# Queries, keys and values of all heads in a first stage, kept in DRAM, instead of a projection inside every head's tiles

## The chip, the cores and the metric

The kernel runs on one core of one Trainium2 chip. The metric is device time in microseconds of one execution, the median of several runs. The trace is of one profiled execution of the kernel before. The granted TensorE clock in it is 1.000 over the whole span.

## The reference

One layer of an encoder over 1024 tokens of width 1024, all in float32. What matters here is branch B, a differential attention of 8 heads, each with two softmax maps of 64 channels and values of 128 channels:

```python
h = rmsnorm(x, g_mix[l])
z = h @ w_in[l]                      # 512 pooling columns | 1024 q | 1024 k | 1024 v
...
qn = head_rmsnorm(q, g_q) * (HEAD_DIM ** -0.5)
kn = head_rmsnorm(k, g_k)
...
    s = jnp.einsum('bqhid,bkhid->bihqk', qblk, kn)
    ...
    s = jnp.where(allowed, s + bias, neg)      # penalty by distance, block-causal mask
    p = jax.nn.softmax(s, axis=-1)
    a = p[:, 0] - lam * p[:, 1]
    return jnp.einsum('bhqk,bkhe->bqhe', a, vf)
...
o = head_rmsnorm(o, g_sub) * (1.0 - lambda_init)
...
gates = jax.nn.sigmoid(h @ w_gate[l] + b_gate[l])
merged = (gates[..., :D_MODEL] * (y_pool @ w_branch_pool[l])
          + gates[..., D_MODEL:] * (y_attn @ w_branch_attn[l]))
x = x + merged @ w_out[l]
```

Branch A is a pooling mixer over the first 512 columns of z. An MLP of width 4096 with a squared ReLU ends the layer.

## The kernel before

Every product of matrices is made of float32r operands that were split in a high and a low part (`split`), and takes three matmuls (`mm3`: hi·hi, hi·lo, lo·hi, lines 123 to 125). Below, z, sc, ta, tk, po, g and u are the names of PSUM tiles, that is, of what a matmul is for.

The tokens are in 8 tiles of 128. x is normalised and transposed to hT (split, kept in SBUF for the whole first part). Then a loop over all 64 pairs of head and tile, numbered g, runs a software pipeline. The string `O = "B1 C2 H6 D3 R7 E4 F5 W-2 A0"` names its stages and how many steps each lags:

- A, `stage_qkv`: the projection z of one tile for one head, 128 tokens by 384 columns (q, k, v of the head): 8 × 3 matmuls of 384 columns.
- B, `stage_prep`: squares and norms of q and k (ACT, DVE, POOL), and V split.
- C, `stage_qkT`: two transposes (tk, line 459) and the splits of K and Q in pieces of 64 partitions.
- D, `stage_scores`: scores sc (lines 499 and 500) in pieces of up to 512 keys. DVE evacuates each piece with the distance penalty and a running minimum (line 502), ACT takes the exponential with its sum (line 510), and DVE forms the coefficient (517, 518) and the difference of the two maps (519).
- E, `stage_aT`: transposes of the weights (ta, line 555), evacuated in halves hi and lo by ACT and DVE (lines 117, 118).
- F, `stage_pv`: the product with V for a pair of tiles (po).
- H, `stage_ssq`: the sum of squares of the outputs, with a 128 × 128 matrix of ones as the moving operand's partner (lines 590, 591) and a DVE pass (593).
- R, `stage_norm`: the factors of one head's outputs, to DRAM.
- W: the loads and splits of the next head's weights, `wqkv`.

A scheduler orders the instructions of each engine from this program. Gate columns (g, 16 units of two halves) and pooling groups (u, yp) are fillers: products without a deadline that are written behind the heads and are moved in where PE would have room. Their results go to DRAM (`g_dram`, `p_dram`). After the heads come the branch projections (bp, ba), w_out (op) and the MLP, itself by a Strassen scheme of seven products, which all stay as they are but for the rooms of some tiles.

## Time and profile before

| | us |
|---|---|
| median of 3 runs | 1554.02 (1553.6 to 1554.59) |
| the profiled execution | 1553.41 |
| its span | 1551.6 |
| PE busy in the span | 1533.6 (99%), 7649 matmuls |
| PEld (weight loads) | 1320.8 (85%) |
| DVE | 1011.3 (65%) |
| ACT | 816.7 (53%) |
| POOL | 354.8 (23%) |

The span goes from the first to the last instruction of the profiled execution; the time has 1.8 us around it. PE is TensorE's multiplies, PEld its weight loads, DVE the VectorE, ACT the ScalarE, POOL GpSimd, SP the engine that issues most of the DMAs. Busy times of matmuls overlap, so the busy time of a group on PE is more than what it takes of the span. In the groups, "out<-in" names the tiles, then come partitions × elements, the count, the busy time and the mean in ns of one, and the idle time ahead with what ended it.

### The profile page before, as it was taken

To read this page: it belongs to the slowest core of one execution; us is meant where nothing else is said; L and a number is where in the kernel's file an instruction comes from. 1 tells how busy PE (TensorE), PEld (TensorE's weight loads), DVE (VectorE), ACT (ScalarE), POOL (GpSimd) and SP (SyncE) were. 2 spreads that over 40 slices of the span, in tenths; PEclk is the share of its full clock that TensorE was granted. 3 is DMA by queue.
4 is the path that set the end of the run, shared out by engine and by line. 5 is a ranking of instruction groups with operands and counts; after the bars stand their busy time and mean duration, and the time that the engine had idled before them with its cause. 6 is when DMAs were issued, how large, how long until landed. Compare 5 with 4: busy or idle time off the path is not lost.

```text
span 1551.6 us, 22088 instructions
## 1 busy us (share of the span) xinstructions
PE 1533.6 (99%) x7649; PEld 1320.8 (85%) x7649; DVE 1011.3 (65%) x2277; ACT 816.7 (53%) x1810; POOL 354.8 (23%) x449
## 2 busy tenths in 40 slices
PE   7999999999999999999999999999999999999999
PEld 6999999999998989888888887888888788888887
DVE  7777677777878787746422458866665667556662
ACT  6656556656566555645532547565555633333331
POOL 5433334243525262324363400000000000000000
PEclk9999999999999999999999999999999999999999
DMA  7111212021202031248536534554343799437650
GB/s 229 51 53 48 66 41 68 24 75 37 75 28 83 28 96 42 69 147 284 179 122 210 168 112 124 182 185 155 129 142 109 278 334 370 170 122 257 224 190 27
DMA packets 168009, 206.94 MB, mean 133 GB/s; under 512 B 10117, under 2 KB 104026, under 8 KB 167898
## 3 DMA queue, kind: packets, MB, share of 16 engines
q1 hardware_dynamic: 150490, 178.23, 35.0%
q10 hardware_dynamic: 17408, 27.30, 4.7%
q8 instruction: 60, 0.98, 0.3%
q14 instruction: 51, 0.42, 0.1%
HBM read 150.94 MB, written 54.56 MB: 132 GB/s over the span
## 4 chain that ended last, share of the span: by engine, by line
PE 89%; DVE 4%; DMA 3%; ACT 1%; issue 1%; POOL 1%; SPq 0%; ACTq 0%; POOLq 0%; DVEq 0%
PE z L125 5%; PE z L123 5%; PE z L124 5%; PE Da L124 4%; PE Da L123 4%; PE Da L125 4%; PE g L123 3%; PE g L124 3%; PE g L125 3%; PE Db L124 3%; PE Db L123 3%; PE Db L125 3%; PE X L125 2%; PE X L123 2%; PE X L124 2%; PE sc L499 2%
## 5 line engine op out<-in xcount | busy, mean ns | idle before, releaser
L123 PE MATMUL z<-wqkv,hT 128*128 128x384 f32 x512 | 174.7, 342 | 0.4 <-DVE qn L441 0.3
L125 PE MATMUL z<-wqkv,hT 128*128 128x384 f32 x512 | 174.3, 341 | 0.5 <-DVE hT L118 0.5
L124 PE MATMUL z<-wqkv,hT 128*128 128x384 f32 x512 | 173.8, 339 | 0.0
L510 ACT ACTIVATE s<-s,nm 128x256 f32<-128x256 f32 (+7 forms) x128 | 99.6, 778 | 49.2 <-DVE nm L502 44.1
L249 POOL TENSOR_TENSOR ms<-ms,mhalf 128x4 f32<-128x4 f32 x64 | 66.6, 1040 | 157.7 <-DVE ms L248 139.1
L125 PE MATMUL g<-hT,fwgate 128*128 128x512 f32 x256 | 101.0, 394 | 0.0
L124 PE MATMUL g<-hT,fwgate 128*128 128x512 f32 x256 | 100.9, 394 | 0.0
L123 PE MATMUL g<-hT,fwgate 128*128 128x512 f32 x256 | 100.9, 395 | 0.0
L123 PEld LDWEIGHTS z<-wqkv,hT 128*128 128x128 f32 x512 | 96.9, 189 | 4.2 <-DVE qn L441 1.0
L125 PEld LDWEIGHTS z<-wqkv,hT 128*128 128x128 f32 x512 | 96.7, 189 | 3.3 <-DVE hT L118 1.3
L124 PEld LDWEIGHTS z<-wqkv,hT 128*128 128x128 f32 x512 | 96.8, 189 | 2.9
L502 DVE CUSTOM_DVE_ANT_0 s<-sc,dist 128x512 f32<-128x512 f32 (+3 forms) x128 | 74.7, 586 | 22.1 <-PE sc L500 20.7
L118 POOL TENSOR_TENSOR wqkv<-rqkv,wqkv 128x384 fp32r<-128x384 f32 x60 | 63.3, 1072 | 17.7 <-ACT wqkv L117 15.3
L499 PE MATMUL sc<-K,Q 128*128 128x512 f32 (+2 forms) x192 | 67.2, 355 | 0.1
L118 DVE TENSOR_TENSOR AS<-s,AS 128x512 fp32r<-128x512 f32 x64 | 43.8, 687 | 35.8 <-ACT AS L117 35.6
L500 PE MATMUL sc<-K,Q 128*128 128x512 f32 (+2 forms) x192 | 66.6, 354 | 0.0
L473 ACT CAST Q<-tk 64x128 fp32r<-64x128 f32 x128 | 33.2, 260 | 58.6 <-DVE Q L472 56.8
L447 POOL TENSOR_TENSOR qn<-qn,ggh 128x128 f32<-128x128 f32 x64 | 32.6, 510 | 137.5 <-DVE qn L441 124.2
L470 ACT CAST Q<-tk 64x128 fp32r<-64x128 f32 x128 | 33.1, 259 | 50.5 <-DVE K L469 49.1
L118 POOL TENSOR_TENSOR fwgate<-frgate,fwgate 128x512 fp32r<-128x512 f32 x32 | 45.2, 1416 | 52.2 <-ACT fwgate L117 52.0
L125 PEld LDWEIGHTS g<-hT,fwgate 128*128 128x128 f32 x256 | 48.1, 188 | 8.6
L123 PEld LDWEIGHTS g<-hT,fwgate 128*128 128x128 f32 x256 | 48.2, 188 | 7.1
(429 smaller groups left out, 4649.6 us busy)
## 6 DMA issues: line engine op xcount, KB each, us to landing
wd<-in_w_down_dram SPq DMA_DIRECT2D x56, 512.0 KB, 5.5
wu<-in_w_up_dram SPq DMA_DIRECT2D x32, 512.0 KB, 5.3
udS<-us SPq DMA_DIRECT2D x64, 256.0 KB, 2.5
ur<-udS SPq DMA_DIRECT2D x32, 512.0 KB, 3.2
rqkv<-in_w_in_dram SPq DMA_DIRECT2D x64, 192.0 KB, 2.8
ud<-u ACTq DMA_DIRECT2D x48, 256.0 KB, 2.2
ur<-ud SPq DMA_DIRECT2D x24, 512.0 KB, 5.5
frgate<-in_w_gate_dram SPq DMA_DIRECT2D x32, 256.0 KB, 2.6
```

What stands on the lines that cost most here:

```text
L118: return (lo_eng or nc.vector).tensor_tensor(lo, src, f(hi), op=ALU.subtract)
L123: nc.tensor.matmul(ps, lhs_hi, rhs_hi, start=first, stop=False, **kw)
L124: nc.tensor.matmul(ps, lhs_hi, rhs_lo, start=False, stop=False, **kw)
L125: nc.tensor.matmul(ps, lhs_lo, rhs_hi, start=False, stop=last, **kw)
L249: nc.gpsimd.tensor_tensor(dst, dst, mhalf[:, :n], op=ALU.pow)
L447: nc.gpsimd.tensor_tensor(qn[:, 2:4, :], qn[:, 2:4, :], ggh.unsqueeze(1).broadcast_to([P, 2, HD]), op=ALU.mult)
L470: nc.scalar.copy(q_hi, q)
L473: nc.scalar.copy(Q[other, m, 1, :], q)
L499: nc.tensor.matmul(dst, Q[:, i, 0, :], rhs, start=True, stop=False)
L500: nc.tensor.matmul(dst, Q[:, i, 1, :], rhs, start=False, stop=True)
L502: nc.vector.tensor_tensor_reduce(out=s[i][:, c : c + w], in0=sc[:, 0:w], in1=dist[:, o0 + c : o0 + c + w], scale=2.0 ** -(h + 1), scalar=B ...
L510: nc.scalar.activation(s[i][:, 0:n], s[i][:, 0:n], AF.Exp, bias=last, scale=-1.0, accum_out=Z[:, i, t : t + 1])
```

## The change

The loop over heads keeps scores, transposes, values' product and norms. What went before them (stages A, B, C, W) becomes a stage of its own, ahead of the heads and for all of them, through DRAM.

- **Values.** For two groups of four heads, each of the 8 tiles takes 24 matmuls of 512 columns. The result is split and stored in `v_dram`.
- **Queries and keys.** q and k of one head are two halves of an output of 256 rows by 1024 tokens; they are computed transposed (channels on partitions) with a scheme of seven products in place of eight. `comb` forms the sums T1 to T4 of quarters of hT once, on DVE, and `qk_pair` forms the sums S1 to S4 of the weights for each head. A product has 4 × 3 matmuls of 512 columns. They are kept in program order on PE (`pin`), two heads interleaved by the string `0111010010011`.
- **Norms.** The squares of a head's q and k are summed over channels with 16 matmuls of plain float32 (not float32r) and 2 columns against `bones`; the factors are transposed, go to DRAM (`rs_dram`) and come back broadcast (`rb`), are multiplied in, and K and Q are split and stored (`k_dram`, `q_dram`). The weights of a head from the fourth on are loaded only after the factors of the head three before it have been loaded.
- **Heads.** `O = "H3 D0 R4 E1 F2 Q-3 W-6"`: K and V come from DRAM six steps ahead (`head_start`), Q for a pair of tiles three steps ahead (`load_q`). The sums of squares of the outputs are two matmuls of plain float32 and 1 column for each pair of tiles. There are three score banks where there were two.
- **Fillers.** A unit u's weights are loaded after the Q load number `FILL(u)`, which spreads the 18 units over the heads' 32 pairs of tiles. They have two banks of their own, where before they had one and, for the last columns, z's. The gate's bias moves from the evacuation into the sigmoid.

The core of the diff:

```diff
-N_Z, N_S, N_T, N_F = 2, 2, 2, 1
+N_S, N_T, N_F = 3, 2, 2
...
+FILL = lambda u: min(max(u - 1, 0) * 4 * H // 18, 4 * H - 1)
...
-O = "B1 C2 H6 D3 R7 E4 F5 W-2 A0"
+O = "H3 D0 R4 E1 F2 Q-3 W-6"
...
+        def values(g, t):
+            th, c0 = t // 4, (t % 4) * P
+            ps = bankA("A", f"v{g}_{t}")
+            for k in range(NK):
+                mm3(
+                    ps, hT[k // 2, th, 0][:, k % 2, c0 : c0 + P], hT[k // 2, th, 1][:, k % 2, c0 : c0 + P],
+                    Wv[g, k][:, 0, :], Wv[g, k][:, 1, :], k == 0, k == NK - 1,
+                )
+            v = t4k(pv, "pb", [P, H // 2, 2, P], F32R, f"V{g}_{t}")
+            src = ps.rearrange("p (a b) -> p a b", a=H // 2)
+            split(v[:, :, 0, :], v[:, :, 1, :], src)
+            nc.scalar.dma_start(v_dram[g][:, :, t], f(v))
...
+                a, b, c = (temp(n) for n in "abc")
+                add(dve, a, f(B12[0]), f(B12[1]))
+                add(dve, b, f(B22[0]), f(B22[1]))
+                sub(dve, c, b, a)
+                keep_T(3, c)
...
+            def product(ps, a, b, more=False):
+                for k in range(4):
+                    mm3(ps, a[:, 0, k, :], a[:, 1, k, :], *operand(b, k), not more and k == 0, k == 3, more, pin)
+
+            with ExitStack() as order:
+                if h > 2:
+                    order.enter_context(tc.issue_after(rb_last[h - 3].ins))
+                (r11, r12), (r21, r22) = load(0), load(1)
...
+                sq = t4k(psq, "sq", [P, 512], F32, f"sq{h}_{th}{c is c2}")
+                nc.scalar.activation(sq, c[:, th, :], AF.Square)
+                o = 16 * (c is c2) + 4 * th
+                for j in range(4):
+                    pin(nc.tensor.matmul(
+                        ps[:, o + j : o + j + 9 : 8], sq[:, j * P : (j + 1) * P], bones, start=True, stop=True
+                    ))
...
+            for s, c in ((1, c2), (0, c1)):
+                rb = t4k(prb, "rb", [P, S], F32, f"rb{h}_{s}")
...
+                nc.sync.dma_start(f(K[i][0:HD]), d[0:4:3].rearrange("m p c -> p m c"))
...
+                nc.sync.dma_start(f(V[i]), v_dram[h // 4][:, h % 4, 4 * i : 4 * i + 4])
...
         def stage_ssq(h, p):
 
-            po, oq, oqs = st.pop((h, p, "o"))
-            nc.tensor.matmul(po[:, 256:512], ones, oqs[:, 0, :], start=True, stop=False)
-            nc.tensor.matmul(po[:, 256:512], ones, oqs[:, 1, :], start=False, stop=True)
...
+            po, oq = st.pop((h, p, "o"))
             for i in range(2):
...
+                nc.tensor.matmul(
+                    po[:, 256 + i : 257 + i], oq[:, i * P : (i + 1) * P], ones, start=True, stop=True
+                )
+            nc.scalar.copy(SS[h][:, 2 * p : 2 * p + 2], po[:, 256:258])
...
+        with ExitStack() as order:
+            if u > 1:
+                order.enter_context(tc.issue_after(q_loads[FILL(u)].ins))
+                order.enter_context(tc.issue_after(dist_set.ins))
+            return fill_cols(src, c0, name)
```

How the order of instructions moves, at three places. First TensorE among the first scores of head 2, in the kernel before (sc2_2_1_0 is head 2, tile 2, map 1, keys from 0; z2_6 is the projection of head 2, tile 6):

```order
L459 MATMUL tk2_3_2381<-identf_90,qn2_3_2270 128x128 x2
L555 MATMUL ta2_1_0_2408<-identf_90,s2_1_2289 128x128 x2
L500 MATMUL sc2_2_1_0_2417<-K2_0_1893,Q2_2_2276 128x384
L125 MATMUL z2_6_2555<-wqkv2_4_1701,hT2_1_1_326 128x384
L123 MATMUL z2_6_2555<-wqkv2_5_1704,hT2_1_0_325 128x384
L124 MATMUL z2_6_2555<-wqkv2_5_1704,hT2_1_0_325 128x384
L125 MATMUL z2_6_2555<-wqkv2_5_1704,hT2_1_1_326 128x384
L590 MATMUL po1_3_2303<-oqs1_3_2346,ones_97 128x256
L123 MATMUL z2_6_2555<-wqkv2_6_1710,hT3_1_0_327 128x384
L124 MATMUL z2_6_2555<-wqkv2_6_1710,hT3_1_0_327 128x384
L125 MATMUL z2_6_2555<-wqkv2_6_1710,hT3_1_1_328 128x384
L591 MATMUL po1_3_2303<-oqs1_3_2346,ones_97 128x256
```

The same place in the changed kernel, the head's tiles 1 to 3:

```order
L704 MATMUL sc2_1_0_0_3475<-Kb2_0_3146,Qb2_0_3287 128x256
L792 MATMUL po1_2_3386<-ones_76,oS1_2_3436 128x1 x2
L703 MATMUL sc2_1_1_0_3501<-Kb2_0_3146,Qb2_0_3287 128x256
L704 MATMUL sc2_1_1_0_3501<-Kb2_0_3146,Qb2_0_3287 128x256
L703 MATMUL sc2_2_0_0_3537<-Kb2_0_3146,Qb2_1_3393 128x384
L704 MATMUL sc2_2_0_0_3537<-Kb2_0_3146,Qb2_1_3393 128x384
L703 MATMUL sc2_2_1_0_3561<-Kb2_0_3146,Qb2_1_3393 128x384
L704 MATMUL sc2_2_1_0_3561<-Kb2_0_3146,Qb2_1_3393 128x384
L703 MATMUL sc2_3_0_0_3572<-Kb2_0_3146,Qb2_1_3393 128x512
L704 MATMUL sc2_3_0_0_3572<-Kb2_0_3146,Qb2_1_3393 128x512
```

The scores of several tiles now follow each other without a projection or a filler between them, and the sum of squares (line 792) is two products of one column. From the first score of head 2 to those of its tile 4 there were 213 rows of TensorE before, and there are 52 now: 24 scores' matmuls, 24 with values of head 1, four rows of transposes and one pair of squares' sums between them.

Second, VectorE in the new stage at the change from the first group of values to the second (comb and T are the sums of hT, wv1_4 is the lower half of the second group's weights for inner block 4, V0_7 that of the last tile's values):

```order
L116 TENSOR_TENSOR T3_01_781<-combc0_776,T3_00_780 128x1024
L116 TENSOR_TENSOR wv1_0_830<-rv1_0_739,wv1_0_830 128x512
L116 TENSOR_TENSOR wv1_1_833<-rv1_0_739,wv1_1_833 128x512
L232 TENSOR_TENSOR combb0_775<-combb0_775,comba0_774 128x1024
L116 TENSOR_TENSOR wv1_2_836<-rv1_1_742,wv1_2_836 128x512
L116 TENSOR_TENSOR wv1_3_839<-rv1_1_742,wv1_3_839 128x512
L229 TENSOR_TENSOR combe0_795<-hT2_0_0_236,hT2_0_1_237 128x1024
L116 TENSOR_TENSOR T1_01_787<-comba0_774,T1_00_786 128x1024
L116 TENSOR_TENSOR wv1_4_845<-rv1_2_842,wv1_4_845 128x512
L116 TENSOR_TENSOR wv1_5_848<-rv1_2_842,wv1_5_848 128x512
L116 TENSOR_TENSOR wv1_6_854<-rv1_3_851,wv1_6_854 128x512
```

The splits of the second group's weights stand among the sums of `comb`; none of this was there before.

Third, SP's queue at the end of the new stage, where the heads' first loads (Qb0 is head 0's Q for a pair of tiles) meet the last head's (rs7, rb7, k7):

```order
L676 DMA Qb0_0_2681<-q0_0_127 64x2x256
L586 DMA rs7_152<-rs7_2575 32x128
L677 DMA Qb0_0_2681<-q0_0_127 64x256
L676 DMA Qb0_0_2681<-q0_0_127 64x2x256
L591 DMA rb7_1_2578<-rs7_152 64x1024 x2
L677 DMA Qb0_0_2681<-q0_0_127 64x256
L676 DMA Qb0_1_2693<-q0_0_127 64x2x256
L677 DMA Qb0_1_2693<-q0_0_127 64x256
L676 DMA Qb0_1_2693<-q0_0_127 64x2x256
L591 DMA rb7_0_2591<-rs7_152 64x1024 x2
L602 DMA k7_0_125<-K7_0_2582 128x2x512
L602 DMA k7_1_126<-K7_1_2587 128x2x512
```

Where SP loaded weights, x and fillers only, it now also has the stores and reloads of q and k between the heads' own loads, and a load behind them is issued after them.

## The prediction, made before the changed kernel was run

> **What bounds the kernel now.** I read the page's head first, then the stretches of the span, then single instructions of TensorE, and at the end the groups of VectorE.

> ```profile
> span 1551.6 us, 22088 instructions
> ...
> PE 1533.6 (99%) x7649; PEld 1320.8 (85%) x7649; DVE 1011.3 (65%) x2277; ACT 816.7 (53%) x1810; POOL 354.8 (23%) x449
> ...
> PE 89%; DVE 4%; DMA 3%; ACT 1%; issue 1%; POOL 1%; SPq 0%; ACTq 0%; POOLq 0%; DVEq 0%
> ```

> PE is busy for 99% of the span, and 89% of the chain that ended last is PE's. The sums below are made against this execution, 1553.41 us (the span and 1.8 us around it); the median of the runs is 1554.02, 0.6 higher. A change of 0.2%, 3 us, is about the least that can be told from none.

> ```profile
> 0.00:40.00 40.00, 30.63 (x168) 27.68 (x168) 28.30 (x68) 25.93 (x64) 23.42 (x50) 1.00 0.73 223
> 100.00:200.00 100.00, 99.36 (x583) 91.90 (x582) 71.34 (x236) 58.45 (x168) 31.76 (x44) 1.00 0.15 47
> 500.00:600.00 100.00, 98.96 (x576) 91.20 (x575) 81.97 (x242) 58.76 (x170) 36.18 (x52) 1.00 0.17 55
> 1400.00:1500.00 100.00, 100.00 (x439) 82.05 (x438) 63.34 (x60) 37.10 (x38) 0.00 (x0) 1.00 0.69 233
> ```

> The columns are the stretch, its us, then PE, PEld, DVE, ACT, POOL, the granted clock, the DMA share and GB/s. Outside the first 40 us PE hardly stops, at full clock, although DVE is 71 to 82% busy. What PE executes is therefore the price, and what DVE, ACT, POOL or the DMA lose is worth nothing by itself. The reader should keep in mind why PE doesn't stop: projection matmuls, which need no engine but PE, stand between any two products of attention.

> **Prices on PE.** Busy times of matmuls overlap, so a price is start to start.

> ```profile
> 399.83 0.34 PE L124 MATMUL z<-wqkv,hT 128*128 128x384 f32 x1
> ...
> 403.65 0.34 PE L125 MATMUL z<-wqkv,hT 128*128 128x384 f32 x1
> ```
> ```profile
> 104.52 0.60 PE L555 MATMUL ta<-identf,s 128*128 128x128 f32 x4
> 104.87 0.42 PE L499 MATMUL sc<-K,Q 128*128 128x384 f32 x1
> 105.13 0.34 PE L500 MATMUL sc<-K,Q 128*128 128x384 f32 x1
> ...
> 111.06 0.29 PE L123 MATMUL po<-AT_0h,V 128*128 128x256 f32 x1
> ...
> 111.90 0.28 PE L124 MATMUL po<-AT_0l,V 128*128 128x256 f32 x1
> ```

> 22 matmuls start between the first two rows: 0.1736 us for 384 columns. 7 between the last two: 0.120 for 256. From the transposes to L500 it is 0.61 us, less 0.174 for L499: 0.109 for each of four. In the stretch 1400 to 1500 there are 439 matmuls of 512 columns without a gap: 0.2278 each.

> **Removed from PE.** The groups give the counts:

> ```profile
> L123 PE MATMUL z<-wqkv,hT 128*128 128x384 f32 x512 | 174.7, 342 | 0.4 <-DVE qn L441 0.3
> ...
> L459 PE MATMUL tk<-identf,qn 128*128 128x128 f32 x128 | 24.4, 272 | 0.0
> ```

> The projection z has this group three times (hi·hi, hi·lo, lo·hi): 1536 × 0.1736 = 266.6. The transposes of q and k: 128 × 0.109 = 14.0. The sums of squares of the outputs, L590 and L591, two of 256 columns for each of 32 pairs of token tiles: 64 × 0.120 = 7.7. Together 288.3 us.

> **Added to PE.** Values: 2 groups of heads × 8 token tiles × 24 = 384 matmuls of 512 columns. Queries and keys: 8 heads × 7 products × 12 = 672 of 512 columns. 1056 × 0.2278 = 240.6. Eight transposes of the norms: 0.9. So Strassen's eighth is there, 96 matmuls or 21.9 us, and the rest of the 26 us between 266.6 and 240.6 is the cheaper column of the wider matmul.

> What is new is 192 products in true fp32 with 1 or 2 columns (128 for the squares of q and k, 64 for those of the outputs). As the kernel is built each becomes two load-and-multiply pairs. No row has one. The nearest:

> ```profile
> 392.92 0.19 PEld L125 LDWEIGHTS g<-hT,fwgate 128*128 128x128 f32 x1
> 393.03 0.19 PEld L123 LDWEIGHTS g<-hT,fwgate 128*128 128x128 f32 x1
> ```

> Two weight loads follow each other here at 0.11 us, which is also the spacing of the transposes, each with a load of its own. I assume that a multiply of 1 or 2 columns hides nothing of the load behind it, and take 2 × 0.11 a product: 192 × 0.22 = 42.2. Below, one load of each might hide: 21.1. Above, the loads might not overlap at all and cost their shown 0.19 each: 73. I take the middle, since four such products stand in a row and only the first load of eight has a wide matmul ahead of it.

> [...] No run here shows such a product yet.

> PE's sum: 240.6 + 0.9 + 42.2 − 288.3 = −4.6 us (from −26 to +26 by the bounds). The branch projections, w_out and the MLP are the same.

> **Work off PE.** Removed: the norm, the splits and the half-width copies of q and k on DVE, ACT and POOL, which lay beside PE's work in the stretches above, so nothing is gained directly. Added: the T matrices, the splits of wider weights, and stores and reloads of q, k and v.

> ```profile
> rqkv<-in_w_in_dram SPq DMA_DIRECT2D x64, 192.0 KB, 2.8
> ```

> Transfers like the new ones land in 2.8 us, and the DMA is 15 to 17% busy where the heads run. K and V are asked for six tiles ahead and Q three, so I cost them at nothing in the middle of the program; without that lead each would cost its 2.8 us. The steady first stage has per head 84 × 0.2278 + 16 × 0.22 = 22.7 us of PE; what the code of one head asks of DVE I put at 16 us (22 operations of 512 columns at 0.67, the split's price below, and four small ones at 0.25, the price of L518 there). PE should run through.

> **New waits.** The projection matmuls are gone from between the scores. Only gate and pooling columns are left to fill, and at four changes of head (1 to 2, 2 to 3, 5 to 6, 6 to 7) none stands between the first tiles of the new head. PE then waits for a score bank that DVE empties:

> ```profile
> L502 DVE CUSTOM_DVE_ANT_0 s<-sc,dist 128x512 f32<-128x512 f32 (+3 forms) x128 | 74.7, 586 | 22.1 <-PE sc L500 20.7
> ...
> L519 DVE SCALAR_TENSOR_TENSOR s<-s,cf,s 128x640 f32<-128x640 f32 (+3 forms) x32 | 35.6, 1112 | 0.6
> L502 DVE CUSTOM_DVE_ANT_0 s<-sc,dist,nm 128x128 f32<-128x128 f32 (+3 forms) x64 | 34.9, 546 | 3.2 <-PE sc L500 1.4
> L118 DVE TENSOR_TENSOR AT_0l<-ta,AT_0h 128x512 fp32r<-128x512 f32 (+1 forms) x48 | 32.0, 666 | 24.6 <-ACT AT_0h L117 23.1 <-PE sc L500 0.8
> ...
> L519 DVE SCALAR_TENSOR_TENSOR s<-s,cf 128x128 f32<-128x128 f32 (+3 forms) x32 | 19.0, 593 | 0.5
> ...
> L518 DVE SCALAR_TENSOR_TENSOR cf<-cf,Z,nlam 128x1 f32<-128x1 f32 x64 | 15.9, 248 | 1.9
> L502 DVE DVE_READ_ACCUMULATOR2_ANT nm<- 128x1 f32 x192 | 15.8, 82 | 0.0
> ...
> L118 DVE TENSOR_TENSOR AT<-ta,AT 128x128 fp32r<-128x128 f32 (+1 forms) x32 | 11.3, 353 | 4.0 <-ACT AT L117 3.8
> ...
> L517 DVE RECIPROCAL cf<-Z 128x1 f32<-128x1 f32 x64 | 10.2, 160 | 25.8 <-ACT s L510 25.2
> ```

> From the first score of head 2 to its tile 4, PE has 8 × 0.228 + 4 × 0.174 + 12 × 0.12 for scores, 24 × 0.12 for values, 11 × 0.109 and 2 × 0.22: 8.5 us. DVE has 10 × 0.586 + 2 × 0.546 + 12 × 0.082 for the same scores, five coefficients at 0.41, four narrow sums at 0.59 and one wide at 1.11, two wide splits at 0.67 and two narrow at 0.35: 15.5 us. Three banks let PE run 3 × 0.59 = 1.8 ahead, and the last sum (1 us) is not waited for: 15.5 − 8.5 − 2.8 = 4 us a place, 16 in all. The lower bound is 0, if PE itself arrives late and DVE has the head start; the upper is 7 × 4 = 28, if DVE arrives with a tile's work undone and nothing runs ahead.

> Entry to the heads: K and Q of head 7 must be multiplied and split (8 operations at 0.67, 5.4 us of DVE) while the first scores want DVE too, and the first Q of head 0 is behind head 7's loads and stores on SP's queue, some two landings of 2.8 us. I take 5, from 0 to 10.

> Change of value group: seven operations of 1024 columns for T (twice 0.67, 1.3) and ten of 512 (0.67) stand ahead of or among the last splits of the weights, 16 us of DVE, beside two tiles of 24 × 0.2278 = 5.5 us of PE: up to 5, I take 3.

> Start: the first weights are 2.0 MB instead of 1.5, at 223 GB/s (first stretch) 2.2 us more; I take 2.

> Sum: −4.6 + 16 + 5 + 3 + 2 = +21.4. 1553.4 + 21.4 = **1575 us**; with half or one and a half of the 26 us of stalls, 1562 to 1588.

> **Rivals.**
> - A, bursts covered. DVE is ahead when a head begins and the waits stay at the 5 us of start and value change: 1553.4 − 4.6 + 5 = 1554, from 1545 to 1560. For it: at 82% DVE busy the old kernel's PE stands still for 1%. Against: there projections lie between the scores. It decides once a place costs under 1 us.
> - B, one load hides. The small products cost 21, the waits as forecast: 1575 − 21 = 1554. Against: they stand four in a row.
> - A and B together: 1533, faster by 1.3%.
> - C, loads that don't overlap: 73 for 42, 1606.
> [...]
> - E, more late transfers: Q is reloaded 32 times; one landing of 2.8 us late in a quarter of them adds 22, 1597.

> **Chances.** Main 0.45, A 0.24, B 0.11, A and B 0.08, C 0.04, D 0.02, E 0.06. Faster by over 0.2%: A and B, 0.13 of A's (its lower half), 0.05 of B's and 0.02 of the main case's tail, 0.28. Within 0.2%: 0.07 of A's, 0.03 of B's, 0.03 of the main case's: 0.13. Slower: 0.59. The range 1540 to 1600 leaves out A and B together, C and D, 0.14, and some of E.

> **What would show it.** Small products: the start-to-start of their loads, 0.11 and two each. Bursts: PE's idle time ahead of scores ended by DVE's evacuation of an older score, in four places. Entry: PE idle ahead of head 0's first scores. If PE is busy over 99% in the heads' stretch, A holds. I am wrong most easily in the bursts, since they rest on an order and a balance of two engines, and in the small products, of which there is no row.

## The result, and the profile after

The changed kernel takes 1606.9 us (median of 4 runs, 1605.71 to 1609.78) against 1554.3, a ratio of 1.0341 (95% interval 1.0323 to 1.0359). It is 53 us slower, where 21 were forecast. Its runs scatter by 4 us and those of its variants by up to 15, so differences under 4 us between variants say little below.

The head of the page after, of an execution of 1607.32 us, and the shares of the chain that ended last:

```profile
span 1605.5 us, 20998 instructions
...
PE 1554.1 (97%) x7369; PEld 1282.2 (80%) x7369; DVE 946.2 (59%) x1741; ACT 762.1 (47%) x1434; POOL 276.2 (17%) x356
...
PE 76%; DMA 9%; DVE 7%; issue 3%; SPq 2%; POOL 2%; ACT 2%; ACTq 0%; DVEq 0%; POOLq 0%
```

Every engine has fewer instructions than before, and all but PE are busy for less time. PE's part of the last chain fell from 89% to 76%: DMA, DVE and SP's queue stand in it now. The stretches that answer to those shown of before, in the same columns, and one stretch of 250 us from the middle of the heads, of before and then of after:

```profile
100.00:200.00 100.00, 98.78 (x483) 82.26 (x482) 52.84 (x92) 41.02 (x74) 24.38 (x13) 1.00 0.36 113
```
```profile
350.00:600.00 250.00, 248.66 (x1444) 229.18 (x1443) 201.18 (x618) 152.25 (x441) 99.03 (x137) 1.00 0.18 57
```
```profile
350.00:600.00 250.00, 244.85 (x1362) 208.38 (x1361) 163.66 (x468) 138.00 (x338) 67.45 (x132) 1.00 0.46 137
```

PE looks as busy as ever. Busy times of matmuls overlap, though, and hide short waits: one of 512 columns is busy for 0.39 us, and the next starts after 0.23. The better reading is the distance from one matmul's start to the next, less the matmul's own spacing (0.2278 us for 512 columns, 0.1736, 0.120 and 0.109 as in the prediction, 0.11 for each row of a small product). Summed over all matmuls, the spacings alone make 1517.4 us before and 1512.7 after, 4.6 less. What lies beyond them is called lost time on PE here, waits and slow matmuls together:

| stretch | before | after | more | forecast |
|---|---|---|---|---|
| start and values (after: to 113 us; before: to 50) | 5.7 | 8.9 | 3.2 | 5 |
| queries and keys (113 to 297) | | 5.9 | | 0 |
| entry to the heads (297 to 349) | | 14.8 | | 5 |
| middle of the heads (349 to 709; before: 50 to 648) | 6.8 | 19.0 | 32.9 with the two rows above | 16 |
| end of the heads and both branch projections (709 to 887; before: 648 to 834) | 2.6 | 23.4 | 20.8 | 0 |
| w_out and MLP | 6.3 | 7.4 | 1.1 | 0 |
| sum | 21.4 | 79.4 | 58.0 | 26 |

−4.6 of work, +58.0 of lost time and +0.6 until the first matmul make the 53.9 us between the spans. The longest waits of PE, in total, times, and longest, in us:

```profile
PE hps L304 <- DVE hn L299: 10.9, 3, 9.4
PE trr L809 <- POOL r L807: 4.9, 1, 4.9
PE sc L703 <- DVE nm L706: 3.9, 3, 3.4
PE ba L121 <- ACT yT L115: 3.1, 2, 2.4
PE ta L760 <- DVE s L723: 2.4, 5, 0.7
PE g L121 <- ACT fwgate L115: 2.4, 4, 1.0
PE po L792 <- ACT oS L783: 2.3, 1, 2.3
PE ss L583 <- POOL ms L560: 2.1, 4, 0.8
```

The reader should see that no wait dominates: the first row is nearly all the start, which before has with 8.8 us, and the other rows are small waits for POOL, DVE and ACT at different places. The last row of them is the transposition that waits for the power of the squares in the first stage. In the middle of the heads alone, 350 to 709 us, the longest rows are:

```profile
PE g L121 <- ACT fwgate L115: 2.2, 3, 1.0
PE ta L760 <- DVE AT_0l L116: 2.1, 4, 0.7
PE ta L760 <- DVE s L723: 2.1, 4, 0.7
PE u L121 <- ACT fwpool L115: 1.0, 1, 1.0
```

These losses stand at certain heads. From a head's first score to its tile 4, the lost time is 2.7, 2.8, 2.7 and 3.0 us at heads 2, 3, 6 and 7, where 0, 29, 0 and 2 filler matmuls stand among them. At heads 1, 4 and 5, with 63, 69 and 43, it is 0.05, 0.06 and 1.0.

About 12 of the 58 us are not waits but slow matmuls. The entry in steps of 2 us, the granted clock being the third number from the right:

```profile
300.00:302.00 2.00, 0.07 (x2) 0.00 (x1) 0.00 (x0) 1.13 (x3) 1.09 (x2) 1.00 0.01 1
302.00:304.00 2.00, 2.00 (x6) 1.61 (x7) 0.00 (x0) 0.61 (x1) 2.00 (x2) 0.67 0.86 225
304.00:306.00 2.00, 2.00 (x10) 1.81 (x9) 0.26 (x1) 0.00 (x0) 1.35 (x2) 0.50 0.98 236
306.00:308.00 2.00, 2.00 (x6) 1.63 (x6) 1.76 (x3) 1.17 (x3) 0.47 (x1) 0.50 0.24 64
308.00:310.00 2.00, 2.00 (x7) 1.61 (x6) 2.00 (x2) 1.54 (x3) 1.73 (x2) 0.62 0.74 217
310.00:312.00 2.00, 2.00 (x11) 1.61 (x10) 1.52 (x3) 0.00 (x0) 1.30 (x2) 1.00 0.88 299
```

After a wait of 1.9 us, which ACT ends behind the cast of a filler's late weights, the clock is at 0.50 for 6.8 us, and the matmuls of 512 columns start 0.43 us apart in place of 0.23. There are five such spells in the execution, of 3.4 to 10.2 us, at waits of 1.9 to 5 us.

### The profile page after: what moved, and what is told of

The parts are those of the page before. It is cut to its first block, busy times and chain, and to the rows that moved or that the text cites. A ratio compares the mean times of both kernels' runs of the same rounds, so it can differ in the third digit from the quotient of the medians.

```text
span 1605.5 us, 20998 instructions
## 1 busy us (share of the span) xinstructions
PE 1554.1 (97%) x7369; PEld 1282.2 (80%) x7369; DVE 946.2 (59%) x1741; ACT 762.1 (47%) x1434; POOL 276.2 (17%) x356
## 4 chain that ended last, share of the span: by engine, by line
PE 76%; DMA 9%; DVE 7%; issue 3%; SPq 2%; POOL 2%; ACT 2%; ACTq 0%; DVEq 0%; POOLq 0%
PE Da L122 4%; PE Da L123 4%; PE Da L121 4%; PE g L121 3%; PE g L122 3%; PE g L123 3%; PE Db L122 3%; PE Db L123 3%; PE X L123 3%; PE Db L121 3%; PE X L122 3%; PE X L121 3%; DMA rb<-rs 2%; PE Z L123 2%; PE Z L122 2%
## 5 line engine op out<-in xcount | busy, mean ns | idle before, releaser
L714 ACT ACTIVATE s<-s,nm 128x128 f32<-128x128 f32 (+7 forms) x128 | 99.0, 776 | 50.1 <-DVE nm L706 47.3
L121 PE MATMUL g<-hT,fwgate 128*128 128x512 f32 x256 | 102.3, 400 | 4.3 <-ACT fwgate L115 2.4
L122 PE MATMUL g<-hT,fwgate 128*128 128x512 f32 x256 | 102.1, 399 | 0.0
L123 PE MATMUL g<-hT,fwgate 128*128 128x512 f32 x256 | 102.1, 399 | 0.0
L560 POOL TENSOR_TENSOR ms<-ms,mhalf 128x8 f32<-128x8 f32 x32 | 60.8, 1903 | 201.7 <-DVE ms L559 201.6
L706 DVE CUSTOM_DVE_ANT_0 s<-sc,dist 128x512 f32<-128x512 f32 (+3 forms) x128 | 72.9, 584 | 11.9 <-PE sc L704 9.4
L703 PE MATMUL sc<-Kb,Qb 128*128 128x512 f32 (+2 forms) x192 | 71.5, 378 | 4.7 <-DVE nm L706 3.9
L704 PE MATMUL sc<-Kb,Qb 128*128 128x512 f32 (+2 forms) x192 | 67.4, 355 | 0.9 <-DMA Qb<-q 0.9
L116 DVE TENSOR_TENSOR AT_0l<-ta,AT_0h 128x512 fp32r<-128x512 f32 (+1 forms) x48 | 31.8, 666 | 57.8 <-ACT AT_0h L115 57.6
L121 PEld LDWEIGHTS g<-hT,fwgate 128*128 128x128 f32 x256 | 48.7, 190 | 15.7 <-ACT fwgate L115 4.0
L123 PEld LDWEIGHTS g<-hT,fwgate 128*128 128x128 f32 x256 | 48.7, 190 | 9.3
L122 PEld LDWEIGHTS g<-hT,fwgate 128*128 128x128 f32 x256 | 48.7, 190 | 9.3
L121 PE MATMUL ba<-yT,wba 128*128 128x512 f32 x128 | 51.5, 404 | 3.1 <-ACT yT L115 3.1
L122 PE MATMUL v<-wv,hT 128*128 128x512 f32 x128 | 50.5, 397 | 1.6 <-DVE wv L116 1.6
L121 PE MATMUL v<-wv,hT 128*128 128x512 f32 x128 | 51.4, 403 | 0.5 <-DVE V L116 0.5
L123 PE MATMUL ba<-yT,wba 128*128 128x512 f32 x128 | 51.7, 404 | 0.0
L122 PE MATMUL ba<-yT,wba 128*128 128x512 f32 x128 | 51.7, 404 | 0.0
L123 PE MATMUL v<-wv,hT 128*128 128x512 f32 x128 | 50.5, 398 | 0.6 <-DVE rs L277 0.6
L122 PE MATMUL op<-wo,mT 128*128 128x512 f32 x128 | 50.0, 393 | 0.9 <-POOL wo L116 0.9
L121 PE MATMUL op<-wo,mT 128*128 128x512 f32 x128 | 50.1, 395 | 0.6 <-ACT wo L115 0.6
```

The costliest lines, as they stand in the source:

```text
L116: return (lo_eng or nc.vector).tensor_tensor(lo, src, f(hi), op=ALU.subtract)
L121: pin(nc.tensor.matmul(ps, lhs_hi, rhs_hi, start=first, stop=False, **kw))
L122: pin(nc.tensor.matmul(ps, lhs_hi, rhs_lo, start=False, stop=False, **kw))
L123: return pin(nc.tensor.matmul(ps, lhs_lo, rhs_hi, start=False, stop=last, **kw))
L560: nc.gpsimd.tensor_tensor(m_, m_, mhalf[:, 0:8].rearrange("p (m t) -> p m t", m=2), op=ALU.pow)
L703: nc.tensor.matmul(dst, Q[:, i, 0, qs], rhs, start=True, stop=False)
```

## The experiments

All are made from the changed kernel unless the text says otherwise, and all times stand against its 1606.9 us. Two theories were tested first: the time is lost at the two ends of the heads' stretch, or in its middle between heads, where fillers are missing. A third came up on the way: the fillers are a fixed stock of cover, and what is lost is lost wherever they don't stand.

**e1, squares of q and k in float32r.**

```diff
-                sq = t4k(psq, "sq", [P, 512], F32, f"sq{h}_{th}{c is c2}")
+                sq = t4k(psq, "sq", [P, 512], F32R, f"sq{h}_{th}{c is c2}")
```

`bones` is float32r too, and the two columns of a product stand side by side in the bank.

> Against the changed kernel, only the 128 products that sum the squares of q and k are in float32r instead of plain float32, so each is one load and multiply instead of two. Theory (a small product costs its weight loads, 0.112 us each on PE, and PE bounds the first stage): 128 x 0.112 = 14 us less, 1593 against 1607. Rival (PE waits in the first stage anyway, and the small products fill waits): less than 4 us. Second rival (the second load of each product was hidden, or the form of the product costs something else): about 0.

1601.0 us (1597.8 to 1605.5), 6 less, between the two expectations. The profiled execution is the slowest of the four. In its PE waits of the first stage (112 to 290 us) stands a part of the rest:

```profile
PE ss L583 <- POOL ms L560: 7.1, 5, 2.0
```

Here the changed kernel itself has 2.1 us. Behind the three longest of these waits the clock is halved for 3.4 us besides. PE's order in the first stage is pinned, and the faster squares brought the transposition to PE before POOL was done.

**e9, the same, with the last squares of a head one product earlier.**

```diff
-            for c in "0111010010011":
+            for c in "0111010100011":
```

> The squares of q and k in float32r as in e1, and the last of the four groups of squares of a head one product earlier in PE's pinned order, so that two products in place of one stand between it and the transposition that waits for POOL's power. Theory (a small product does cost its two loads, and e1 gave back 10 of its 14 us because the transposition came to PE before POOL was done): the waits for POOL in the first stage go below 3 us and the time to 1590 to 1595, 12 to 16 us under 1607. Rival (the first stage is held by something else than PE's work): as e1, about 1601.

1591.4 us (1589.5 to 1599.4), 15.5 less, about the 14.3 that the price of 128 × 0.112 gives. The mechanism agrees only in part: the profiled execution is the slowest of the four, and in it the waits for POOL are gone, but PE waits nearly as long on DVE's pass over the squares in their place:

```profile
PE ss L552 <- DVE ms L559: 6.0, 6, 2.0
```

So the price of the small products is settled by the trace of the changed kernel better than by e9:

```profile
156.34 0.95 PE L552 MATMUL ss<-bones,sq_1True 128*128 128x2 f32 x8
157.15 0.47 PE L121 MATMUL B<-T,A 128*128 128x512 f32 x1
```

Four products of one line of the program are eight rows, that is, two pairs of a load and a multiply each, 0.112 us apart (the median of all 256 for the squares). That is 0.22 a product, as taken: each product of 2 columns has two rows in the trace, and the time of two. What a wide product in plain float32 takes, no run here shows.

**e2, the last head without its own factors.**

```diff
-                        rb[halves[m], :], rs_dram[h][2 * s + m].partition_broadcast(HD)
+                        rb[halves[m], :], rs_dram[min(h, H - 2)][2 * s + m].partition_broadcast(HD)
```

> Leaves out that the last head's q and k get their own factors: they are multiplied by those of the head before it, which have been in DRAM for long, so no round trip of the factors through DRAM stands at the end of the first stage. All instructions stay. Theory of the ends (DVE's queue is held by the last head's multiply, which waits for its factors, ahead of the first scores' evacuation, and PE's clock is halved for some 6 us after a wait of over 2 us): the waits of 3.5 and 1.5 us at 331 to 336 and the half-clock spell behind them go, 6 to 9 us less. Theory of the middle (the stalls come from the stretches between heads without fillers): 0.

1612.8 us (1611.4 to 1615.3), 6 more. The wait on DVE at 331 did go, but the scheduler, which sees the factors ready early, put the last head's stores ahead of head 0's loads of Q on SP's queue, and the first scores then waited 4.3 us for those loads. The entry costs 19.9 us instead of 14.8. Not a proof against DVE's queue as the holder in the changed kernel, but taking that one hold away is worth nothing.

**e11, a room of its own for the last factors.**

```diff
-                rb = t4k(prb, "rb", [P, S], F32, f"rb{h}_{s}")
+                rb = t4k(*((pr, "raw") if h == H - 1 and not s else (prb, "rb")), [P, S], F32, f"rb{h}_{s}")
```

> The factors of the last head's q get a room of their own, so their load doesn't wait until the last head's k has been multiplied. Theory of DVE's queue (the multiply of the last q waits for its factors ahead of the first scores' evacuation): the wait of 3.5 us at 331 and the spell behind it shrink, 3 to 6 us less. Rival (SP's queue, on which head 0's Q loads stand behind the last head's stores): 0 to 2 us.

1623.0 us (1621.7 to 1625.1), 16 more. A miss for both expectations. In PE's waits between 295 and 370 us:

```profile
PE sc L703 <- DMA Qb<-q: 9.3, 3, 6.0
```

The first score comes at 336 instead of 326, again behind Q's loads. The middle is worse too, 30 us of lost time for 19.

**e7, stores of q and k on ACT's queue.**

```diff
-                    nc.sync.dma_start((q_dram, k_dram)[s][h][th].rearrange("l p c -> p l c"), f(t))
+                    nc.scalar.dma_start((q_dram, k_dram)[s][h][th].rearrange("l p c -> p l c"), f(t))
```

> The stores of q and k are issued on ACT's queue instead of SP's. Theory of SP's queue at the entry (head 0's first loads of Q stand behind stores that wait for DVE, and each issue takes SP 0.6 us): the first scores start some 4 us earlier and the waits among them shrink, 4 to 8 us less. Rival (the first scores wait for DVE, whose queue is held by the last head's multiply): 0 to 2.

1609.1 us (1606.3 to 1611.5): no gain, entry 14.4 for 14.8. SP's queue is not the one holder of the entry either.

**e10, three fillers instead of two at the entry.**

```diff
-FILL = lambda u: min(max(u - 1, 0) * 4 * H // 18, 4 * H - 1)
+FILL = lambda u: min(max(u - 2, 0) * 4 * H // 17, 4 * H - 1)
...
-            if u > 1:
+            if u > 2:
```

> Three units of gate columns in place of two may run before the heads' first Q; the rest is spread over the same stretch. Theory of the entry (27 us pass between the last product of the first stage and the first score, and two fillers of 11 us each and their weights are all that PE has): the excess of 15 us around the entry falls by 5 to 8, and the time by as much. Rival (the fillers are a fixed stock, and what is spent here is missing later): the entry falls and the middle or the end rises by as much, 0 in sum.

1617.5 us (1613.5 to 1621.9), 11 more. The entry does fall, from 14.8 to 6.0 us of lost time, somewhat more than the 5 to 8 expected; the middle rises from 19.0 to 34.4. What is spent at the entry is missing later, with interest: the rival expected 0 in sum.

**e3, the last two fillers late.** They are issued behind the last head's exponentials on ACT.

```diff
+LATE = {18: (7, 7), 19: (7, 7)}
...
+            if u in LATE:
+                order.enter_context(tc.issue_after(exps[LATE[u]].ins))
```

> The last two units of gate columns (22 us of PE) are held until the last head's last exponentials; nothing else. Theory of the ends (fillers run out 5 us before the last scores, the last head's chain of scores, transposes, values, norm has no cover, and the branch projections are spent as cover so that the attention projection comes before its operands): the waits of 2.1, 2.5, 5.1 and 3.4 us from 725 to 811 and their half-clock spells go for the larger part, 10 to 18 us less. Theory of the middle: the two units are missing between the heads 6 and 7 instead, where PE then waits more; 0 or slower by up to 8 us.

1607.5 us (1604.9 to 1612.1): nothing. The transposition of the last norms comes at 743 instead of 762, without a long wait, but PE stands still before it (698 to 724) and behind it in the attention projection (at 811). The longest of these waits is for the late fillers' own weights:

```profile
PE g L122 <- ACT fwgate L116: 4.1, 1, 4.1
```

**e4, the third weights of the attention projection once.**

```diff
-        elif d > NK - 4:
+        elif d > NK - 3:
```

> Behind the heads, the third of the attention projection's weight columns is loaded once instead of twice (the kernel before loads it twice as well), which takes one load of 512 KB and two splits from SP's, ACT's and POOL's queues. Theory of the ends, in the form that SP's queue held the last loads of the heads' outputs behind weight loads that waited for POOL: the wait of 2.6 and 0.9 us at 807 and the spell of half clock behind it go, 5 to 7 us less. Rival (those loads are late since the last head is late): 0 to 1 us.

1608.2 us (1603.3 to 1614.0), no change that the scatter would show.

**e5, the attention projection's weights behind all outputs of the heads.** The load of those weights moves from the loop over d behind it.

```diff
-        elif d > NK - 4:
-            j = len(ws_ba)
-            ws_ba[j] = load_cols(w_branch_attn, j * P, f"ba{j}")
...
+    for j in range(2):
+        ws_ba[j] = load_cols(w_branch_attn, j * P, f"ba{j}")
     mT = {}
```

> Behind the heads, the first weights of the attention projection are loaded behind all loads of the heads' outputs (and the third no longer twice), so that on SP's queue no load of an output stands behind a weight load that waits for POOL. Theory of SP's queue (in order, its weight loads wait for rooms that POOL frees, and the outputs of head 6 are issued only at 803, which PE waits for at 807): the wait inside the attention projection and its half-clock spell go, 6 to 9 us less than 1607. Rival of the late last head (the chain of head 7 ends at 762 and sets the end of this stage, whatever stands on the queue): 0 to 2 us, with another wait at the same place.

1603.1 us (1601.7 to 1605.7), 3.8 less, at the edge of what the scatter would show. The wait inside the attention projection is gone and its half-clock spell with it; the last head comes later in this execution (769 for 762) and takes a part back. That SP's queue stood there is in its waits of the changed kernel, 715 to 825 us:

```profile
SPq L153 <- POOL wba L116: 23.7, 7, 7.8
SPq L194 <- DVE yT L116: 12.8, 3, 9.8
```

L153 is the weights' load, L194 that of the heads' outputs behind it.

**e6, both edits at the end** (e3 and e5).

> Both edits at the heads' end: the last two units of gate columns are held until the last head's exponentials, and the attention projection's weights are loaded behind all outputs. If the end of this stage has two limits that replace each other (PE's cover for the last head, which e3 took away without gain, and SP's queue), both edits together give what neither gives alone: 12 to 20 us less than 1607. Rival of the middle: 0 to 8, as e3 and e5.

1599.5 us (1595.1 to 1602.8), 7.4 less: more than either, but less than the 12 to 20 forecast and within the rival's 0 to 8. The end's lost time goes from 23.4 to 16.7, and what is left stands before the last head's end, where the two fillers were; 4.1 of it is again the wait for their own weights. The variants that don't touch the end have between 15.6 (e7) and 24.4 us (e10) there, so this number alone proves little.

**e8, four banks for scores.**

```diff
-N_S, N_T, N_F = 3, 2, 2
+N_S, N_T, N_F = 4, 2, 1
```

> Four banks for scores and one for fillers, instead of three and two. Theory of the middle (PE waits in the runs of scores without fillers because DVE frees score banks late): the excess of 19 us between 350 and 700 shrinks by a third to a half, 6 to 10 us less. Theory of the ends: the excess in the middle changes by less than 4 us, and 4 us or less in all; one filler bank may cost some of it again, since a filler's bank is evacuated by ACT before the next can start.

1610.8 us (1606.9 to 1621.6), not faster; the middle's lost time is 24.5 for 19.0. Score banks are not what PE waits for in the middle, whether or not the single filler bank costs something.

**e12, products that nobody reads where PE waits.** 12 and 24 matmuls of 512 columns ahead of the last sum of squares and the last transposition.

```diff
+            warm(12)
             for i in range(2):
...
+            warm(24)
```

> 36 products of 512 columns that nobody reads are put on PE just ahead of the last head's sum of squares (12) and just ahead of the transposition of its norms (24), where PE waited for 2.5 and 5.1 us. If a wait of over 2 us is what halves the clock: no half-clock spell from 755 to 768, while the transposition still comes at about the same time, 762. If the clock is halved by something else (the number of weight loads, the DMA): the spell stays. The time changes by under 3 us either way.

1605.5 us (one run). The same 4 us stretches from 756, of the changed kernel and then of e12:

```profile
756.00:760.00 4.00, 0.99 (x4) 0.90 (x4) 2.85 (x4) 1.31 (x4) 1.26 (x1) 0.58 0.16 57
760.00:764.00 4.00, 1.54 (x5) 1.25 (x6) 1.69 (x4) 1.68 (x4) 1.85 (x2) 0.50 0.57 154
764.00:768.00 4.00, 4.00 (x13) 3.14 (x12) 0.71 (x1) 2.15 (x2) 0.00 (x0) 0.64 0.30 114
```
```profile
756.00:760.00 4.00, 3.40 (x17) 2.48 (x15) 0.10 (x1) 0.74 (x2) 0.41 (x2) 1.00 0.01 4
760.00:764.00 4.00, 4.00 (x18) 3.31 (x19) 0.60 (x1) 0.03 (x1) 0.00 (x0) 1.00 0.44 132
764.00:768.00 4.00, 4.00 (x20) 3.30 (x19) 0.00 (x0) 1.70 (x3) 1.29 (x1) 1.00 0.00 0
```

With work on PE the clock stays at 1.00, and the transposition is at 759. So at this place it is the wait that halves the clock. The time itself is within the scatter.

**e13 to e15, an eighth of the fillers' work.** By now edits that took a wait away at one place had brought it back at another. The next three change the amount of cover and nothing else.

```diff
-        for k in range(NK):
+        ks = [0, 1, 2, 3, 4, 5, 6]
+        for n, k in enumerate(ks):
```

e14 has `[0, 1, 2, 3, 4, 5, 6, 7, 0]`, and e15 is e13's edit in the kernel before.

> Leaves out the last eighth of the inner dimension in every filler (gate columns and pooling channels): 20 units x 2 halves x 3 matmuls x 0.228 = 27 us of PE less, spread evenly. Theory of a fixed stock of cover: the heads' chains run as long as before and PE waits more, so the time falls by only 10 to 18 us from 1607. Rival (separate waits on queues and transfers): it falls by 25 to 28.

> Every filler repeats its first eighth of the inner dimension: 27 us of PE more, spread evenly (the gates and pooling channels are wrong by it). Theory of a fixed stock of cover: a part of the 27 fills waits, so the time rises by only 8 to 18 us from 1607. Rival: it rises by 25 to 28.

> The kernel before with the last eighth of the inner dimension of every filler left out: 27 us of PE less. There PE is busy 99% and never waits among the heads, so both theories expect the whole of it: 1554 - 27 = 1527, give or take 2.

| 27 us of PE work | time | change |
|---|---|---|
| e13, less, changed kernel | 1603.5 (1598.4 to 1607.9) | −3.4 |
| e14, more, changed kernel | 1619.2 (1615.8 to 1624.7) | +12.3 |
| e15, less, kernel before | 1547.9 (1546.9 to 1550.3), ratio 0.9959 (0.9944 to 0.9973) | −6.6 |

In the changed kernel e14 meets the theory of a fixed stock (8 to 18), e13 neither theory's number; the rival's 25 to 28 is refuted on both sides. In e13 the clock took a part. From the first score to the last it is halved for 30.9 us, against 6.8 in the changed kernel; the matmuls that no wait separates lost 11.9 us by it, against 1.9. That stretch of the changed kernel and then of e13:

```profile
326.00:728.80 402.80, 386.42 (x2123) 325.43 (x2122) 257.66 (x747) 224.47 (x552) 107.58 (x200) 0.99 0.50 150
```
```profile
326.00:726.60 400.60, 373.21 (x1997) 309.83 (x1995) 256.56 (x743) 222.46 (x550) 106.45 (x200) 0.96 0.51 151
```

e15 is the surprise: both theories expected 27 us, and the kernel before, whose PE is busy 99%, gives 6.6. Its heads take as long as they did, 622 us from the first score to the last for 620, because the order has nearly as many fillers among them, 181 us of their matmuls for 185. What was left out is missing behind the last score: 5 us of fillers there for 28. The last head's outputs are done at 696 (693 before), and PE waits for its norms once:

```profile
PE trr L611 <- POOL r L609: 12.3, 1, 12.3
```

**e17 and e18, seven eighths left out**, in the changed kernel and in the kernel before (`ks = [0]`).

> Every filler of the changed kernel does one eighth of its products: 20 x 2 x 21 x 0.228 = 191 us of PE less, evacuations and loads as before. If the heads' chains (scores, DVE, exponentials, transposes, values) run at a pace of their own that lies just under what PE needs, the time falls by 30 to 80 us and PE waits the rest. If PE's work set the pace and the waits came from queues and transfers, it falls by 150 or more.

> The same in the kernel before: 191 us of PE less. Its heads carry the projections besides, so if their own pace lies just under PE's work (e15), the time falls by 30 to 80 us as well, with the projections between the scores now waiting like the rest; if e15's small gain came only from the one wait at the end of the last head (12 us), it falls by 120 or more.

191 us of PE work less are worth 77 us in the changed kernel (1530.2, 1529.3 to 1531.1) and 50 in the one before (1503.8, 1501.0 to 1506.5), both inside the 30 to 80 of heads with a pace of their own. From the first score to the last it is 339 us for 403 in the changed kernel and 591 for 620 before. 350 to 600 us of e17 and then e18:

```profile
350.00:600.00 250.00, 200.06 (x1041) 158.99 (x1042) 190.44 (x558) 165.50 (x417) 78.36 (x157) 0.87 0.59 175
```
```profile
350.00:600.00 250.00, 223.73 (x1303) 203.80 (x1301) 202.01 (x684) 152.35 (x471) 82.62 (x124) 0.97 0.11 34
```

In e17 no engine is full: PE 80%, part of it at half clock, DVE 76%, ACT 66%. That points to the chain through PE, DVE, ACT and back as the pace, not to one engine. But between the first score and the last the clock is halved for 107 of e17's 339 us and for 51 of e18's 591, so a part of this pace is the clock's. How fast the chains would go at full clock, no run here shows.

**e16, what paid, together** (e9 and e6).

> The edits that paid, together: squares in float32r one product earlier (e9, 15.5 us), the last two units of gate columns late and the attention projection's weights behind the outputs (e6, 7.5 us). If they act at different places they add: 1584. If the gain of the first is eaten by the stock of fillers at the end: 1588 to 1592. The kernel before, 1554, is not reached either way.

1590.6 us (1586.1 to 1592.5): no better than e9 alone, and in the range for a gain that is eaten by the stock of fillers. Nothing tried here comes near the kernel before.

## Why the prediction was wrong

**PE's sum was right.** −4.6 us of work was forecast, and the matmuls in the traces at the prediction's own spacings give −4.6. That confirms the counts. The one new price, 0.22 us for a small product, is the measured one; the rivals with one load and with loads that don't overlap are refuted by two rows a product, 0.112 us apart. Rival D, with 0.02 of the chances, asked for four loads a product, which no run shows; the runs show the two rows.

**The terms that were mis-sized are the waits: 26 us forecast, 58 measured.**
- Start and value change, 2 and 3: together 3.2. Right in size, and 1.6 of it is the wait for DVE's split of the second group's weights, as argued.
- Entry, 5, from 0 to 10: 14.8 in the stretch around it. Two holds were named (DVE and SP's queue), and e2, e7 and e11 show that taking one away leaves the other in its place. Two half-clock spells, some 5 us, were not in the sum.
- Bursts, 16 at four places: 19.0 in the middle, or 12 more than before if all of its 6.8 are set against it. The places are right: 11 us are lost at the four changes of head that the prediction named, 2.7 to 3.0 at each where it had 4, and rival A, which asked for under 1 us a place, is refuted. What PE waits for there is only in part what was argued. It is DVE, but the scores' waits for it are 3.9 us over the whole execution, nearly all of it at the entry, and four score banks (e8) gained nothing. The losses are waits of 1 us or less of the transposes for DVE's differences and splits, and of the next filler for its weights.
- Steady first stage, "PE should run through": 5.9 us lost. It was costed at nothing since DVE's 16 us a head fit in PE's 22.7; left out was POOL's power and PE's pinned order behind it, 2.1 of the 5.9 (e1).
- End of the heads, not in the sum at all: 20.8. This is the largest miss. "The branch projections, w_out and the MLP are the same", says the prediction, and prices no wait there.
- Rival E, late transfers: refuted. All waits of scores for Q's loads are 1.3 us.

**So the waits failed: the end was put at nothing, and the entry at a third of what it took. The step behind that is the first one: "What PE executes is therefore the price, and what DVE, ACT, POOL or the DMA lose is worth nothing by itself."** It was read from a PE at 99%. e15 shows that 27 us of PE work less were worth only 6.6 in that same kernel: the fillers left out had covered the end of its last head, and PE lost 21 us more, 12 of them in one wait there. e18 left out 191 us, and the time fell by only 50. A sum over PE finds what PE executes; it can't find a limit that lies just under it. The busy shares don't show it either: that of the matmuls goes only from 99% to 97%. That of the weight loads (PEld) goes from 85% to 80%, but in part because there are 280 loads fewer, and its 85% before is no measure of PE's room either: start to start only 21.4 us, 1.4% of the span, were lost. The kernel before hid its last head behind fillers, and that could be read from its trace. Its last score and its last filler, then those of the changed kernel:

```profile
668.50 0.40 PE L500 MATMUL sc<-K,Q 128*128 128x512 f32 x1
...
700.80 0.39 PE L125 MATMUL g<-hT,fwgate 128*128 128x512 f32 x1
```
```profile
722.30 0.40 PE L123 MATMUL g<-hT,fwgate 128*128 128x512 f32 x1
...
728.80 0.40 PE L704 MATMUL sc<-Kb,Qb 128*128 128x512 f32 x1
```

In the kernel before, fillers ran on for 32 us behind the last score (28 us of matmuls); in the changed kernel they end 6 us ahead of it. The projections had been cover for the heads, 266 us of it, 246 behind the first score, and the change moved that work into a stage of its own, where it covers nothing. The prediction saw this between the heads and not at their end, although the orders of both kernels show it.

What stays open: which link of the heads' chain sets its pace, and how much of it the halved clock does. e8, e17 and the engines' shares speak against score banks and a full engine; DMA latency, the rooms of K and V and the written order were not separated. No run gave the changed kernel its cover back, so that the missing cover accounts for the whole of the 58 us is not shown. The edits that paid take 16 us off together (e16), 14 of them by less work on PE, and leave 77 us lost on PE. That the rooms which K and V keep until the end delay the branch projections' loads is argued from the code; no run changed them alone.

## What to carry to other kernels

An engine that is busy 99% is not proof that its work is the price (27 us of PE work less gave 6.6 us here, e15): before work is moved away from beside a chain of dependent steps, ask how fast that chain would go alone, and measure it by leaving filler work out. Work without a deadline is a stock; count it, look what it covers behind the last step, and see that a change which takes cover away is charged with it. Edits that remove one wait at a time are worth little while the cover stays too small.

## What the runs showed of the hardware

In the changed kernel a product in plain float32 with 1 or 2 columns is two pairs of a load and a multiply (256 rows for the 128 of the squares, 128 for the 64 of the outputs), 0.112 us apart in the median. The two weight loads that the prediction shows at 392.92 and 393.03 us stand as close; that the loads set this time is argued, not tested.
